# Branch projections, output projection and down product in rounds of four jobs, with pieces that roll through SBUF

## The chip, the cores and the metric

One core of a Trainium2 chip runs the whole kernel in one launch. The metric is the device time of that launch in microseconds. Five engines work side by side, each through its own queue in order: TensorE (PE in the profile, its weight loads PEld), VectorE (DVE), ScalarE (ACT), GpSimd (POOL) and SyncE (SP), which here issues the DMAs. SBUF is the memory on the chip, PSUM the eight banks that TensorE writes to, HBM the memory outside.

## The reference

One decoder layer on x, 1024 tokens by 1024 channels, float32:

```python
h = rmsnorm(x, norm_mix[l])
proj = h @ w_in
...
ys = jnp.stack([y_gla, y_mlstm, y_fox], axis=2)
branch = jnp.einsum('btnw,nwd->btnd', ys, w_branch)
g = jax.nn.sigmoid(gates.reshape(bsz, seq, N_BRANCH, D_MODEL) + b_gate)
merged = jnp.sum(branch * g, axis=2)
return merged @ w_out
...
h = rmsnorm(x, norm_ffn[l])
u = causal_dwconv(h @ w_up, conv_w, conv_b)
a, g = jnp.split(u, 2, axis=-1)
return (jax.nn.silu(g) * a) @ w_down
```

Both halves are added to x, and a last rmsnorm follows. Three token mixers (gated linear attention, mLSTM, forgetting attention) make the three ys from proj. The FFN's inner width is 2816, 22 blocks of 128.

## The kernel before

A large matrix product is a GEMM in jobs. A job takes 256 output channels: a two by two block product done with seven products instead of eight (Strassen in Winograd's form), numbered 1 to 7. Its stationary sides are a11, a12, a22 and four sums of blocks of the weights; its moving sides, the pieces, are two by two blocks of the activations and four differences of them. Every float32 operand is split into a high part (a cast on ScalarE) and a low part (a subtraction on VectorE, L151), and a product is three matmuls per 128 rows of depth: high by high, low by high, high by low. With four such depths a product has 12 matmuls of 128x512 and a job 84. `prep` (L1120) makes a product's weight sum on GpSimd (L1127) and splits it; it runs AHEAD = 2 products before `compute` (L1146), which does the matmuls (L143) and hands the PSUM bank to the job's `post` or `acc`. `products` (L51) sets the order: the seven products of a job, with products 3 and 4 of the job before between them.

From the start to some 1380 us run 48 input jobs and the mixers. Then come three branch GEMMs of four jobs (`merge_job` L1063: gate times branch output, summed over the branches into the tiles mg), the output projection (`out_half` L1261: plain, 768 matmuls of 256 columns, with the merged tiles split by `merged_split` L1082 as stationary), 22 up jobs, and the down product in three chunks of the inner width (6, 8 and 8 blocks) of four jobs each, added in SBUF into the rows acc (L1334).

The pieces of a branch or down GEMM are made by `combos` (L1022), a generator of seven steps. Each step loads blocks (tiles yb, T), takes differences (L1038, L1043, L1051, L1059; on VectorE, for the first chunk of down on GpSimd) and splits them into the slots b0 to b27. Step i hangs on the end of the i-th product of the last job of the GEMM before (`hook` L1362), so all seven fall into one job's time. A slot is written again once the last job has read the piece in it.

The norm at the start scales rows and turns them in one go: matmuls of x by a diagonal matrix dg (L226, `turn4` L229). The FFN norm turns rows that are already scaled (L1289, L147).

Each engine works through its queue in order, SP with its DMAs too, in an order fixed at build time; an instruction that waits holds up all behind it. A pool that is opened after another was closed takes its space: a first write to it waits until the last reader of the old tile is done.

Of the kernel before, what the change touches and what calls it, by code (L numbers as in the profile page):

```python
# [14 lines left out]
P = 128  # L15
T = 1024
# [19 lines left out]
MAP_IN = {1: 0, 5: 4, 6: 8, 2: 12, 7: 16, 3: 20, 4: 24}  # L36
MAP_FF = {1: 16, 2: 20, 5: 24, 6: 0, 7: 4, 3: 8, 4: 12}
# [3 lines left out]
class Job:  # L41
# [3 lines left out]
    def __init__(self, src1, src2, xc, post, name, nk=4, done=None, wide=False, acc=None):  # L45
        self.src, self.xc, self.post, self.name, self.nk = (src1, src2), xc, post, name, nk
        self.done, self.wide, self.acc = done, wide, acc
        self.raw, self.w, self.after = None, {}, {}

# [35 lines left out]

class Kern:
    def __init__(self, ctx, tc, a):
# [7 lines left out]
        self.swp = ctx.enter_context(tc.tile_pool(name="swp", bufs=1, reuse_waits="tile"))  # L95

# [39 lines left out]
    def slot(self, i, shape, dt, name):  # L136
        return self.big.tile(shape, dt, tag=f"b{i}", name=name)
# [14 lines left out]

    def unit(self, src, name="w"):
        raw = self.swp.tile([P, T], F32, tag="raw", name=f"{name}_raw", bufs=4)
        self.nc.sync.dma_start(out=raw, in_=src)
        out = []
        for i in range(2):
            hi = self.swp.tile([P, 512], F32R, tag="sh", name=f"{name}h", bufs=4)
            lo = self.swp.tile([P, 512], F32R, tag="sl", name=f"{name}l", bufs=4)
            self.split(raw[:, 512 * i:512 * i + 512], hi, lo)  # L160
            out.append((hi, lo))
        return out
# [52 lines left out]
    def norm(self, x, pool, vec):  # L215
# [9 lines left out]
        dg = pool.tile([P, P], F32, tag="dg", name="dg", bufs=4)  # L225
        nc.vector.tensor_scalar(dg, self.ident, sm[:, 2:3], None, op0=ALU.mult)  # L226
        return x, dg

    def turn4(self, xs, k):  # L229
        ps = self.pa()  # L230
        for i, x in enumerate(xs):
            o = ps[:, i * P:(i + 1) * P]
            if isinstance(x, tuple):
                self.mm(o, x[0][:, k * P:(k + 1) * P], x[1], True, True)
            else:
                self.tr(o, x[:, k * P:(k + 1) * P])
        return ps
# [14 lines left out]
    def put(self, xc, n, i, src, base, eng=None):  # L252
        t = self.slot(base[n] + i, [P, 2, 512], F32R, f"x{n}_{i}")
        self.split(src, t[:, 0, :], t[:, 1, :], eng)
        xc.setdefault(n, {})[i] = (t[:, 0, :], t[:, 1, :])

    def blocks1(self, xs, b, pool, gain, xc, base, qpool, qtag):
# [1416 lines left out]
```

## Time and profile before

| | |
|---|---|
| median of 3 runs | 2469.17 us (2462.83 to 2472.13) |
| profiled execution | 2460.64 us, span 2458.5 us |
| granted TensorE clock, mean | 0.983 |
| TensorE busy | 2333.9 us, 95% |
| VectorE busy | 1856.2 us, 75% |
| ScalarE busy | 1246.0 us, 51% |
| GpSimd busy | 903.8 us, 37% |
| DMA | 334.53 MB, 136 GB/s on the mean |

A busy share near 100% says that an engine always had something in hand, not that each instruction was as short as it can be; matmuls overlap, so their own durations sum to more than the time they take. What counts is the distance from one start to the next.

### The profile page before, as it was taken

How to read it: one execution, taken by the hardware profiler on the slowest of the kernel's cores; microseconds unless marked ns; L12 is line 12 of the kernel's file. 1: busy time of each engine (PE TensorE's matmuls, PEld its weight loads, DVE VectorE, ACT ScalarE, POOL GpSimd, SP SyncE). 2: the span in 40 equal slices, each digit the busy share in tenths (PEclk: the TensorE clock that was granted, in tenths of full speed). 3: DMA queues.
4: the chain of work that ended last, by engine and by line, in shares of the span. 5: the costliest groups of instructions: out<-in, count | busy, mean ns of one | idle time of the engine just before them, and what ended most of it. 6: DMA issues, size and time to landing. Idle time of an engine off the chain costs nothing. (4 is left out here: it accounts for less than half of the span.)

```text
span 2458.5 us, 34199 instructions
## 1 busy us (share of the span) xinstructions
PE 2333.9 (95%) x11531; PEld 1933.2 (79%) x11531; DVE 1856.2 (75%) x3180; ACT 1246.0 (51%) x2477; POOL 903.8 (37%) x892
## 2 busy tenths in 40 slices
PE   7999999989999999999999999899989999988898
PEld 6877778878888887888888777679878888876776
DVE  7687556767677775666778788864699998999885
ACT  5345455555566654555555643434455455553342
POOL 5322244444354452222222234551254433443322
PEclk9999999999999999999999999899989999999999
DMA  3355444554434444333443655434332222235442
GB/s 127 114 173 173 137 138 148 173 163 164 156 134 143 140 142 143 123 131 120 136 130 109 210 180 177 163 116 164 124 112 85 79 77 95 78 113 190 142 133 86
DMA packets 185743, 334.53 MB, mean 136 GB/s; under 512 B 17320, under 2 KB 79304, under 8 KB 185056
## 3 DMA queue, kind: packets, MB, share of 16 engines
q1 hardware_dynamic: 185568, 332.35, 40.9%
q8 instruction: 91, 1.49, 0.3%
q14 instruction: 84, 0.69, 0.1%
HBM read 236.70 MB, written 95.58 MB: 135 GB/s over the span
## 5 line engine op out<-in xcount | busy, mean ns | idle before, releaser
L143 PE MATMUL pg<-x,w6h 128*128 128x512 f32 x744 | 239.0, 400 | 12.7 <-DVE x L151 11.1
L143 PE MATMUL pg<-x,w7h 128*128 128x512 f32 x744 | 235.4, 397 | 2.6 <-ACT u L1155 2.5
L143 PE MATMUL pg<-x,w1h 128*128 128x512 f32 x744 | 236.0, 397 | 0.1
L143 PE MATMUL pg<-x,w4h 128*128 128x512 f32 x744 | 231.9, 392 | 3.1 <-DVE mt L1074 2.2
L143 PEld LDWEIGHTS pg<-x,w6h 128*128 128x128 f32 x744 | 140.4, 192 | 46.6 <-DVE x L151 15.3
L1127 POOL TENSOR_TENSOR sum<-up_raw 128x512 f32<-128x512 f32 x44 | 87.4, 1986 | 242.6 <-DMA up_raw<-in_w_up 201.0
L143 PE MATMUL pg<-x,w1l 128*128 128x512 f32 x372 | 148.7, 400 | 17.5 <-DVE w1l L151 17.5
L143 PEld LDWEIGHTS pg<-x,w7h 128*128 128x128 f32 x744 | 138.8, 191 | 33.1 <-ACT u L1155 4.6
L143 PEld LDWEIGHTS pg<-x,w4h 128*128 128x128 f32 x744 | 137.8, 188 | 33.1 <-issue 3.3
L143 PEld LDWEIGHTS pg<-x,w1h 128*128 128x128 f32 x744 | 140.0, 191 | 28.8 <-DVE x L151 0.5
L143 PE MATMUL pg<-x,w7l 128*128 128x512 f32 x372 | 147.2, 396 | 3.8 <-DVE w7l L151 3.8
L143 PE MATMUL pg<-x,w6l 128*128 128x512 f32 x372 | 147.1, 395 | 0.0
L143 PE MATMUL pg<-x,w4l 128*128 128x512 f32 x372 | 145.2, 390 | 1.0 <-DVE w4l L151 1.0
L1303 DVE SCALAR_TENSOR_TENSOR c<-u,cols,c 128x1022 f32<-128x1022 f32 x84 | 129.6, 1543 | 12.3 <-ACT c L1299 12.3
L150 ACT CAST w5h<-sum 128x512 fp32r<-128x512 f32 (+1 forms) x94 | 57.8, 615 | 131.0 <-PE pg L143 85.9
L143 PE MATMUL pg<-x,w5h 128*128 128x512 f32 x384 | 123.5, 401 | 0.4 <-DVE st L1234 0.3
L143 PE MATMUL pg<-x,w2h 128*128 128x512 f32 x384 | 121.6, 398 | 0.4 <-DVE st L1234 0.4
L143 PE MATMUL pg<-x,w3h 128*128 128x512 f32 x384 | 121.3, 395 | 0.0
L151 DVE TENSOR_TENSOR w5l<-sum,w5h 128x512 fp32r<-128x512 f32 (+1 forms) x94 | 87.9, 935 | 41.7 <-ACT w5h L150 35.4
L143 PE MATMUL pa<-x,w5h 128*128 128x512 f32 x360 | 114.4, 399 | 1.8 <-ACT w5h L150 0.9
L143 PE MATMUL pa<-x,w2h 128*128 128x512 f32 x360 | 111.2, 390 | 2.9 <-ACT w2h L150 2.9
L143 PE MATMUL pa<-x,w3h 128*128 128x512 f32 x360 | 113.7, 398 | 0.0
(481 smaller groups left out, 6881.3 us busy)
## 6 DMA issues: line engine op xcount, KB each, us to landing
up_raw<-in_w_up SPq DMA_DIRECT2D x44, 512.0 KB, 3.6
yb<-y_d SPq DMA_DIRECT2D x72, 256.0 KB, 3.5
yb<-in_w_dn SPq DMA_DIRECT2D x66, 256.0 KB, 3.2
gate_raw<-in_w_in SPq DMA_DIRECT2D x24, 512.0 KB, 3.6
g_d<-st SPq DMA_DIRECT2D x48, 256.0 KB, 2.2
br_raw<-in_w_br SPq DMA_DIRECT2D x24, 512.0 KB, 4.5
gth<-g_d SPq DMA_DIRECT2D x48, 256.0 KB, 2.6
f_d<-c SPq DMA_DIRECT2D x22, 512.0 KB, 2.9
```

The source lines that it names most:

```text
L143: self.nc.tensor.matmul(out, lhsT=lhsT, rhs=rhs, start=start, stop=stop, skip_group_check=skip)
L150: self.nc.scalar.copy(out=hi, in_=src)
L151: (eng or self.nc.vector).tensor_tensor(out=lo, in0=src, in1=hi.bitcast(F32), op=ALU.subtract)
L1127: self.nc.gpsimd.tensor_tensor(out=t, in0=a, in1=b, op=op)
L1303: nc.vector.scalar_tensor_tensor(out=c[:, s:], in0=u[:, :T - s], scalar=self.col("fw", 44 * tap + m), in1=c[:, s:], op0=ALU.mult, op1=ALU.add)
```

## The change

- The start norm scales x in place (rows in turns on VectorE and ScalarE) and turns it by PE transposes; the diagonal goes.
- Pieces live in seven groups of four tiles (g0 to g6). Branch GEMMs take five groups in rotation, the down chunks seven.
- Branch GEMMs, the output projection and the first two down chunks run in rounds: one product for all four jobs, then the next, in the order 1, 2, 5, 6, 3, 7, 4. Their weights lie in SBUF at once (pools `swp` and `wide`), their sums are made in place. The third chunk keeps the old order.
- A piece step hangs on the end of a round, about four rounds ahead of its use in the branches. For the branches after the first, differences 5 and 6 are on VectorE, 7 and 4 on GpSimd; for the first branch, the output projection and down all are on GpSimd.
- The output projection has four jobs of seven products, 336 matmuls of 512 columns; merged tiles are the stationary side, blocks of w_out the pieces, and x rows take the sum. `merged_split` and `out_half` go; `row_norm` does the norm of whole rows.
- The eight acc tiles are all in one pool that opens at the end of the FFN; the first adds wait for their loads.

```diff
+ORDER = (1, 5, 6, 2, 7, 3, 4)
+ROUND = (1, 2, 5, 6, 3, 7, 4)
+ROLL_BR = (0, 1, 2, 3, 4)
+ROLL_DN = (3, 0, 1, 4, 2, 5, 6)
...
+def rounds(jobs, ps=ROUND):
+
+    for p in ps:
+        for j in jobs:
+            yield j, p
...
+    def group(self, g, dt, name):
+
+        return self.big.tile([P, 4, 2, 512] if dt is F32R else [P, 4, T], dt, tag=f"g{g}", name=name)
...
-        dg = pool.tile([P, P], F32, tag="dg", name="dg", bufs=4)
-        nc.vector.tensor_scalar(dg, self.ident, sm[:, 2:3], None, op0=ALU.mult)
-        return x, dg
+        if vec:
+            nc.scalar.activation(x, x, AF.Copy, scale=sm[:, 2:3])
+        else:
+            nc.vector.tensor_scalar(x, x, sm[:, 2:3], None, op0=ALU.mult)
+        return x
     def turn4(self, xs, k):
         ps = self.pa()
         for i, x in enumerate(xs):
-            o = ps[:, i * P:(i + 1) * P]
-            if isinstance(x, tuple):
-                self.mm(o, x[0][:, k * P:(k + 1) * P], x[1], True, True)
-            else:
-                self.tr(o, x[:, k * P:(k + 1) * P])
+            self.tr(ps[:, i * P:(i + 1) * P], x[:, k * P:(k + 1) * P])
...
+    def combos(self, n, block, xc, base, order, ytile, ttile, engs):
+
...
+        for p in order:
+            for i in range(n):
+                if p == 1:
+                    src = load(0, i, 0)
+                elif p == 2:
+                    src = load(1, i, 0)
+                elif p == 3:
+                    src = load(1, i, 1)
+                elif p == 5:
+                    b = load(0, i, 0)
+                    src = ts[i] = ttile(i)
+                    nc.sync.dma_start(out=src, in_=block(0, i, 1))
+                    engs[p].tensor_tensor(out=src, in0=src, in1=b, op=ALU.subtract)
+                elif p == 6:
+                    b = load(1, i, 1)
+                    src = ts[i]
+                    engs[p].tensor_tensor(out=src, in0=b, in1=src, op=ALU.subtract)
+                elif p == 7:
+                    src = load(0, i, 0)
+                    engs[p].tensor_tensor(out=src, in0=ts[i], in1=src, op=ALU.subtract)
+                else:
+                    src = load(1, i, 0)
+                    engs[p].tensor_tensor(out=src, in0=src, in1=ts[i], op=ALU.subtract)
+                self.put(xc, p, i, src, base)
...
+    def out_job(self, env, p, xc, rows, done):
+
         nc = self.nc
+
+        def load(job):
+            mg = env["mg"]
+            for i in range(2):
+                rows[2 * p + i] = r = self.raw_tile(job, "x2")
+                nc.sync.dma_start(out=r, in_=self.a["x"][(2 * p + i) * P:(2 * p + i + 1) * P, :])
+            return [mg[kh][:, :, (2 * p + i) * P:(2 * p + i + 1) * P] for i in range(2) for kh in range(2)]
+
+        def acc(m, hf, b):
+            o = rows[2 * p + m][:, 512 * hf:512 * hf + 512]
+            nc.vector.scalar_tensor_tensor(out=o, in0=b, scalar=0.5, in1=o, op0=ALU.mult, op1=ALU.add)
+        return Job(None, None, xc, None, "wo", wide=True, acc=acc, load=load, done=lambda: done(p))
 
...
-            elif p == 7:
-                acc(1, 1, job.z)
+            elif p == 5 or p == 7:
                 acc(1, 1, b)
             elif p == 4:
...
+    def row_norm(self, pool, x, tt):
+        nc = self.nc
+        sm = pool.tile([P, 3], F32, tag="sm", name="sm", bufs=4)
+        junk = pool.tile([P, D], BF16, tag="junk", name="junk", bufs=1)
+        nc.sync.dma_start(out=self.x2_d[tt], in_=x)
+        nc.scalar.activation(junk, x, AF.Square, accum_out=sm[:, 0:1])
+        self.rsqrt(sm[:, 2:3], sm[:, 0:1], 1.0 / D, sm[:, 1:2], 1)
+        nc.vector.tensor_scalar(x, x, sm[:, 2:3], None, op0=ALU.mult)
...
+    def down_job(self, p, k0, nk, acc, wait, xc):
         nc = self.nc
 
         def add(m, hf, b):
-            o = acc[2 * p + m][:, 512 * hf:512 * hf + 512]
-            nc.vector.tensor_tensor(out=o, in0=o, in1=b, op=ALU.add)
+            def run():
+                o = acc[2 * p + m][:, 512 * hf:512 * hf + 512]
+                nc.vector.tensor_tensor(out=o, in0=o, in1=b, op=ALU.add)
+            if acc:
+                run()
+            else:
+                assert b is not None and hf == 0 and m == 0
...
+                jobs = wide([k.merge_job(env, n, b, p, x) for p in range(4)])
+                gemm.append((jobs, list(rounds(jobs)), x, branch_blocks(b),
+                             {5: V if n else G, 6: V if n else G, 7: G, 4: G}))
+            x = {}
+            jobs = wide([k.out_job(env, p, x, rows, ready.append) for p in range(4)])
+            seq = [(jobs[i], p) for h in ((0, 1), (2, 3)) for p in (1, 2) for i in h]
+            seq += list(rounds(jobs, (5, 6)))
+            seq += list(rounds(jobs[0:2], (3, 7, 4))) + list(rounds(jobs[2:4], (3, 7, 4)))
+            gemm.append((jobs, seq, x, out_blocks, {5: G, 6: G, 7: G, 4: G}))
+            steps, ends = [], []
+            m = 0
+            for jobs, seq, x, blocks, engs in gemm:
+                base = {}
+                for p in ROUND:
+                    base[p] = ROLL_BR[m % 5]
+                    m += 1
+                gen = k.combos(4, blocks, x, base, ROUND, ytile, ttile, engs)
+                steps += [gen] * 7
+                for p in ROUND:
+                    ends.append([q for q in seq if q[1] == p][-1])
+            for i, gen in enumerate(steps):
+                job, p = (ins[-1], ORDER[i]) if i < 5 else ends[i - 5]
+                after(job, p, lambda gen=gen: next(gen))
+            yield from products(ins, LEADS)
+            yield None, 0
+            for jobs, seq, x, blocks, engs in gemm:
+                for j in jobs:
+                    j.held = env["wide"]
+                yield from seq
...
+                last = c == len(chunks) - 1
+                x = {}
+                ds = [k.down_job(p, k0, nk, acc, wait, x) for p in range(4)]
+                ps = ORDER if last else ROUND
+                base = {p: ROLL_DN[i] for i, p in enumerate(ps)}
+                gen = k.combos(nk // 2, dn_blocks(c), x, base, ps,
+                               lambda: k.swp.tile([P, 512], F32, tag="ws", name="yb", bufs=3),
+                               lambda i: k.swp.tile([P, 512], F32, tag="sc", name="T", bufs=4),
+                               {5: G, 6: G, 7: G, 4: G})
+                steps += [gen] * 7
+                if last:
+                    for p, j in enumerate(ds):
+                        j.second = p % 2 == 1
+                        j.done = lambda p=p: dn["done"].extend((2 * p, 2 * p + 1))
+                    seqs.append((ds, products(ds)))
+                else:
+                    wide(ds)
+                    seqs.append((ds, rounds(ds)))
+                    ends += [(ds[-1], p) for p in ROUND]
+            for gen, (job, p) in zip(steps, ends):
...
             nfin = ep.tile([P, D], F32, name="nfin")
-            for i in range(2, 8):
+            for i in range(8):
                 acc.append(ep.tile([P, D], F32, name=f"acc{i}"))
-                k.nc.sync.dma_start(out=acc[i], in_=k.x2_d[i])
-            k.nc.sync.dma_start(out=nfin, in_=a["norm_final"].partition_broadcast(P))
-            dn["done"] = []
+                nc.sync.dma_start(out=acc[i], in_=k.x2_d[i])
+            for f in wait:
+                f()
```

VectorE in the middle of the branches, first before, in the last job of the first branch: x7 and the like are pieces, w3l and the like low parts of weights, mt and mg belong to the merge.

```order
L1051 TENSOR_TENSOR yb_16238<-T_16061,yb_16238 128x512
L1077 SCALAR_TENSOR_TENSOR mg7_15647<-gth_16233,mt_16235 128x512
L1051 TENSOR_TENSOR yb_16244<-T_16067,yb_16244 128x512
L151 TENSOR_TENSOR x7_0_16241<-yb_16238,x7_0_16241 128x512
L1051 TENSOR_TENSOR yb_16250<-T_16073,yb_16250 128x512
L151 TENSOR_TENSOR x7_1_16247<-yb_16244,x7_1_16247 128x512
L1051 TENSOR_TENSOR yb_16256<-T_16079,yb_16256 128x512
L151 TENSOR_TENSOR x7_2_16253<-yb_16250,x7_2_16253 128x512
L151 TENSOR_TENSOR w3l_16265<-sum4_16262,w3h_16264 128x512
L151 TENSOR_TENSOR x7_3_16259<-yb_16256,x7_3_16259 128x512
L151 TENSOR_TENSOR w6l_16286<-sum2_16283,w6h_16285 128x512
L151 TENSOR_TENSOR w4l_16305<-br_raw_15952,w4h_16304 128x512
```

Now, in the round of product 3 of the second branch:

```order
L1076 TENSOR_TENSOR mt_16671<-u2_16576,pa_16466 128x512
L166 TENSOR_TENSOR w7l_16700<-sum1_16389,w7h_16699 128x512
L1079 SCALAR_TENSOR_TENSOR gth_16669<-gth_16669,mt_16671 128x512
L1076 TENSOR_TENSOR mt_16694<-u2_16595,pa_16487 128x512
L166 TENSOR_TENSOR w7l_16723<-sum1_16414,w7h_16722 128x512
L1079 SCALAR_TENSOR_TENSOR gth_16692<-gth_16692,mt_16694 128x512
L1051 TENSOR_TENSOR T_16746<-T_16746,yb_16744 128x512
L1051 TENSOR_TENSOR T_16754<-T_16754,yb_16752 128x512
L1076 TENSOR_TENSOR mt_16717<-u2_16614,pa_16507 128x512
L1051 TENSOR_TENSOR T_16761<-T_16761,yb_16759 128x512
L1079 SCALAR_TENSOR_TENSOR gth_16715<-gth_16715,mt_16717 128x512
L1051 TENSOR_TENSOR T_16768<-T_16768,yb_16766 128x512
```

Before, four differences, their four splits and a single job's weights stand in one product after another; now the merge of four jobs, four weights and four differences of a single piece group share a round.

SP at the start of the down product, before (acc0 and acc1 stand 90 rows earlier):

```order
L1314 DMA f_d_115<-c_22428 128x1024
L1027 DMA yb_22951<-in_w_dn 128x512
L1314 DMA f_d_115<-c_22633 128x1024
L1115 DMA dn_raw_22781<-f_d_115 128x6x128
L1535 DMA acc2_22689<-x2_d_114 128x1024
L1535 DMA acc3_22691<-x2_d_114 128x1024
L1535 DMA acc4_22693<-x2_d_114 128x1024
L1535 DMA acc5_22695<-x2_d_114 128x1024
L1535 DMA acc6_22697<-x2_d_114 128x1024
L1535 DMA acc7_22699<-x2_d_114 128x1024
```

and now:

```order
L1310 DMA f_d_115<-c_22000 128x1024
L1036 DMA yb_22109<-in_w_dn 128x512
L1036 DMA yb_22114<-in_w_dn 128x512
L1036 DMA yb_22118<-in_w_dn 128x512
L1601 DMA acc0_22060<-x2_d_114 128x1024
L1601 DMA acc1_22062<-x2_d_114 128x1024
L1601 DMA acc2_22064<-x2_d_114 128x1024
L1601 DMA acc3_22066<-x2_d_114 128x1024
L1601 DMA acc4_22068<-x2_d_114 128x1024
```

The loads of acc stood behind the last f_d store for six rows; now for all eight, and three piece loads stand between.

VectorE around the first add into acc, now (the last f, L1309 on tile c, stands five rows ahead of the first row; x4 and x1 are pieces of the first and second chunk):

```order
L166 TENSOR_TENSOR x4_21986<-yb_21989,x4_21986 128x512
L166 TENSOR_TENSOR x4_21986<-yb_21994,x4_21986 128x512
L166 TENSOR_TENSOR w5l_22159<-sum1_22156,w5h_22158 128x384
L166 TENSOR_TENSOR x1_22111<-yb_22109,x1_22111 128x512
L166 TENSOR_TENSOR w5l_22176<-sum1_22173,w5h_22175 128x384
L166 TENSOR_TENSOR x1_22111<-yb_22114,x1_22111 128x512
L166 TENSOR_TENSOR w5l_22210<-sum1_22207,w5h_22209 128x384
L166 TENSOR_TENSOR x1_22111<-yb_22118,x1_22111 128x512
L1331 TENSOR_TENSOR acc0_22060<-acc0_22060,pg_22018 128x512
L166 TENSOR_TENSOR w5l_22227<-sum1_22224,w5h_22226 128x384
L1331 TENSOR_TENSOR acc0_22060<-acc0_22060,pa_22130 128x512
L1331 TENSOR_TENSOR acc2_22064<-acc2_22064,pg_22043 128x512
```

Before, five adds into acc0 and acc1 stood ahead of the last f; now the first add stands 13 rows behind it, and the adds of four jobs follow together.

## Rows read from the trace of the kernel before

**Rows 1.** The page: busy us of each engine, share of the span, instructions

```profile
PE 2333.9 (95%) x11531; PEld 1933.2 (79%) x11531; DVE 1856.2 (75%) x3180; ACT 1246.0 (51%) x2477; POOL 903.8 (37%) x892
```

**Rows 2.** Stages: us, TensorE busy (instructions), granted clock, DMA share, GB/s

```profile
1380.00:1659.00 279.00, 253.73 (x1068) 0.97 0.52 170
1659.00:1760.00 101.00, 97.29 (x799) 1.00 0.47 163
1760.00:1803.00 43.00, 33.56 (x140) 0.84 0.09 32
1803.00:2165.00 362.00, 362.00 (x1599) 1.00 0.28 93
2165.00:2440.00 275.00, 249.00 (x1032) 0.96 0.43 137
```

**Rows 3.** TensorE in time, output projection: start us, us, operation

```profile
1744.78 0.28 PE L143 MATMUL pg<-woh,mh 128*128 128x256 f32 x1
1744.90 0.28 PE L143 MATMUL pg<-wol,mh 128*128 128x256 f32 x1
```

**Rows 4.** TensorE in time, entry of the FFN; last, a stage

```profile
1771.17 4.23 PE L147 MATMUL pa<-cst,x 128*128 128x128 f32 x32
...
1785.18 0.63 PE L143 MATMUL pg<-x,w6l 128*128 128x512 f32 x1
1785.61 0.63 PE L143 MATMUL pg<-x,w6h 128*128 128x512 f32 x1
...
1784.00:1798.00 14.00, 8.20 (x17) 0.52 0.00 0
```

**Rows 5.** Waits of TensorE, branches: us in total, times, longest us

```profile
PE pa L143 <- DVE w5l L151: 4.6, 1, 4.6
```

**Rows 6.** Waits of TensorE, down product

```profile
PE pg L143 <- DVE w1l L151: 11.3, 5, 3.9
```

**Rows 7.** Stages: VectorE busy us (instructions); last, GpSimd

```profile
1380.00:1659.00 279.00, 230.19 (x312) 0.97 0.52 170
1820.00:2160.00 340.00, 309.88 (x288) 1.00 0.27 92
2165.00:2440.00 275.00, 237.70 (x316) 0.96 0.43 137
...
1380.00:1659.00 279.00, 128.88 (x79) 0.97 0.52 170
```

**Rows 8.** VectorE in time; GpSimd in time beside it; VectorE later without it

```profile
1781.10 1.76 DVE L273 TENSOR_TENSOR t<-b,t 128x512 f32<-128x512 f32 x1
1782.78 1.75 DVE L151 TENSOR_TENSOR x<-t,x 128x512 fp32r<-128x512 f32 x1
...
1782.28 1.71 POOL L284 TENSOR_TENSOR b<-b,t 128x512 f32<-128x512 f32 x1
...
1797.78 0.68 DVE L151 TENSOR_TENSOR w5l<-sum,w5h 128x512 fp32r<-128x512 f32 x1
1798.38 0.68 DVE L151 TENSOR_TENSOR w3l<-sum,w3h 128x512 fp32r<-128x512 f32 x1
```

**Rows 9.** SP in time, loads of acc; last, their landing

```profile
2233.92 0.33 SPq L1314 DMA_DIRECT2D f_d<-c  x1
...
2234.90 3.32 SPq L1535 DMA_DIRECT2D acc<-x_d  x6
...
DMA to landing us min/median/max: 2.6/2.7/9.6
```

**Rows 10.** VectorE in time, convolution at the end of the FFN

```profile
2226.33 1.27 DVE L1303 SCALAR_TENSOR_TENSOR c<-u,cols,c 128x1022 f32<-128x1022 f32 x1
```

**Rows 11.** TensorE in time, start; last, a later VectorE group

```profile
10.28 10.52 PE L143 MATMUL pa<-dg,x 128*128 128x128 f32 x64 [10.28 <-DVE dg L226]
...
35.73 4.80 PE L143 MATMUL pa<-dg,x 128*128 128x128 f32 x26 [2.94 <-DVE dg L226]
...
L1289 DVE TENSOR_SCALAR x<-x,sm 128x1024 f32<-128x1024 f32 x6 | 4.5, 752 | 7.9 <-DMA x_d<-x 7.6 <-POOL sm L167 0.3
```

More of the change, by code (lines that the diff above doesn't have):

```diff
@@ L1194, in compute, with gemms @@
             f()
-    def gemms(self, jobs, lead=0):
-        seq = products(jobs, lead)
+    def gemms(self, seq):
         due = []
@@ L1394, in body, with ytile @@
[L1394 to L1405 removed]
+        env = {}
+        rows = {}
+        V, G = nc.vector, nc.gpsimd
+        def ytile():
+            return env["cmb"].tile([P, 512], F32, tag="yb", name="yb", bufs=4)
@@ L1443, in body @@
                 pass
-        with pool("mrg") as gp:
-            mrg["pool"] = gp
-            while ("g", 23) not in k.written:
-                next(stream)
-            stage.close()
-            gr = right.enter_context(pool("mg", side="right"))
-            mrg["mg"] = mg = [gr.tile([P, T], F32, name=f"mg{j}") for j in range(8)]
-            for _ in stream:
-                pass
-            k.merged_split(mg, (6, 7), mh, ml)
-        right.close()
+        env["wide"] = k.raw2 = left.enter_context(pool("wide"))
+        env["cmb"] = cmb.enter_context(pool("cmb"))
+        while ("g", 23) not in k.written:
+            next(stream)
+        stage.close()
+        late = ctx.enter_context(ExitStack())
+        env["late"] = late.enter_context(pool("late", side="right"))
+        env["mg"] = [k.group(g, F32, f"mg{g}") for g in (5, 6)]
+        for _ in range(3 * 28):
+            next(stream)
+        late.close()
+        lp = right.enter_context(pool("lead", side="right"))
         xc = {}
-        lp = right.enter_context(pool("lead", side="right"))
         bg = []
@@ L1483, in ffn @@
         def ffn():
             jobs = list(k.ffn_jobs(xc, tiles, bg))
-            last = jobs[-1]
+            seqs, steps, ends = [], [], [(jobs[-1], p) for p in ORDER]
             for c, (k0, nk) in enumerate(chunks):
-                hook(last, Lazy(lambda c=c: down_combos(c, xcs[c])))
-                for p in range(4):
-                    jobs.append(k.down_job(p, k0, nk, acc, xcs[c]))
-                    if c == len(chunks) - 1:
-                        jobs[-1].done = lambda p=p: dn["done"].extend((2 * p, 2 * p + 1))
-                last = jobs[-1]
@@ new lines, in ffn @@
+            yield from products(jobs, LEADS)
+            for ds, seq in seqs:
+                for job, p in seq:
+                    if p not in (1, 2):
+                        job.held = dn["pool"]
+                    yield job, p
+        ff = k.gemms(ffn())
+        for _ in range(12):
+            next(stream)
+        cmb.close()
+        with pool("oh", side="right") as hp:
+            while len(ready) < 2:
+                next(stream)
+            for tt in range(4):
+                k.row_norm(hp, rows[tt], tt)
+            next(stream)
+            b = k.blocks0([rows[tt] for tt in range(4)], hp, "nf")
+            next(stream)
+            for p in (1, 2):
+                for i in range(4):
+                    k.put(xc, p, i, b[i + 4 * (p - 1)], MAP_FF)
+            for _ in stream:
+                pass
+            for tt in range(4, 8):
+                k.row_norm(hp, rows[tt], tt)
+            for _ in range(2 * LEADS):
+                next(ff)
+            for _ in k.blocks1([rows[tt] for tt in range(4, 8)], b, hp, "nf", xc, MAP_FF,
+                               lambda i: k.swp.tile([P, 512], F32, tag="sc", name="b22", bufs=4),
+                               lambda i: env["wide"].tile([P, 512], F32, tag="S", name="t1", bufs=4)):
+                pass
```

295 lines of the change are left out of this document (104 added, 191 removed).

## Prediction, written before the result was known

> **What bounds the kernel now.** I read the busy shares first, then a table of stages, then TensorE's waits in the stages that the change touches, and last single rows for prices. TensorE is busy 95% of a span of 2458.5 us, VectorE 75% [rows 1]. That is an average over stages. In the table of stages [rows 2] the up projection of the FFN, 1803 to 2165 us, is filled: 1599 matmuls in 362.0 us, never idle, so one 512-column matmul costs 362.0/1599 = 0.2264 us. With that price the other stages show what they lose:
> - branches, 1380 to 1659 us: 279.0 - 1068 x 0.2264 = 37.2 us;
> - down product, 2165 to 2440: 275.0 - 1032 x 0.2264 = 41.4 us;
> - output projection, 1659 to 1760: its 256-column matmuls follow each other every 0.12 us [rows 3], so 768 x 0.12 = 92.2 us, and 32 transposes at 4.23/32 = 0.13 us [rows 4] make 4.2; 101.0 - 96.4 = 4.6 us lost;
> - entry of the FFN, 1760 to 1803: 43.0 - 108 x 0.2264 - 4.2 = 14.3 us.
> In branches and down product TensorE waits for VectorE's low halves of weights (w5l, w1l) [rows 5, 6], and VectorE is busy 230.2 of 279 and 237.7 of 275 us [rows 7]. The piece steps all hang on the last job of the GEMM before, so VectorE's work comes in heaps while its average fits.
>
> **The change part by part.**
> Branches. TensorE's work stays (12 jobs x 84 matmuls; a branch is 336 x 0.2264 = 76.1 us). On VectorE a branch now has 28 subtractions for pieces, 28 for weights, 28 in the merges, and 8 piece differences in the first two branches: 92, 92, 84. GpSimd has 24, 40 and 48 operations (16 weight sums, 8 or 16 piece differences, 16 merge adds from the second branch on). Back to back a VectorE operation comes every 0.60 us [rows 8]. What one GpSimd operation adds to VectorE I take from the stage itself: 312 operations x 0.60 = 187.2 of the 230.2 us busy, so 43.0/79 = 0.54 us each [rows 7]. That gives 55.2 + 13.0 = 68.2, 55.2 + 21.6 = 76.8 and 50.4 + 25.9 = 76.3 us against 76.1: 0.9 us over. Rounds are uneven (the one of p3 and the one of p7 carry 16 to 24 VectorE operations in 12 x 4 x 0.2264 = 10.9 us), but pieces run four rounds ahead and weights three products, so I book 3 us a branch, 9. At each of the two boundaries between branches 4 MB of weights come within about two rounds (21.7 us), beside pieces and gates of some 5 MB; DMA moved 170 GB/s at a share of 0.52 [rows 2], so 327 GB/s when full, and 9 MB take 27.5 us; most has a round to spare, and I book 3 us each, 6. Lost 16 instead of 37.2: **gain 21**. Ends: 6 lost (gain 31) if the lead hides the unevenness; at the dearest row for GpSimd beside VectorE [rows 8], where one operation of each takes 1.68 us together (1782.78 - 1781.10), the price is 1.68 - 0.60 = 1.08 us, VectorE needs 81.1, 98.4 and 102.2, that is 53.4 over TensorE, 68 lost (gain -31). I take 0.54, since it is the mean of these very operations.
>
> Output projection. 336 matmuls x 0.2264 = 76.1 us for 92.2: 16.1 less. The moving pieces are made during the last branch (counted above), the split of the merged tiles (16 operations on VectorE) goes, and its stationary is cast like any weight. Without the merged split the start has no chain of its own; I book 3 us lost for 4.6. **Gain 17.7**; ends 12 (a chain through the last merge, as long as the longest wait of rows 5, twice) and 20.
>
> Entry of the FFN. The norm now is one Square of 1024 and one scaling of 1024 per row instead of four pieces, and blocks1 stays: 32 transposes, then a chain of VectorE and GpSimd in turns at half TensorE clock (0.52) [rows 4]. I see no operation leave this chain, so 14.3 stay; ends 10 and 20. **Gain 0**.
>
> Down product. Its piece differences go to GpSimd: of 316 VectorE operations 32 leave, 284 x 0.60 = 170.4; GpSimd has 48 sums and 44 differences, x 0.54 = 49.7; 220 us against 1032 x 0.2264 = 233.6, so on average VectorE is no bound (at 1.08 it would be 269.8, 36 over). What stays is the start. All eight acc tiles now share a pool that opens when the FFN's is released, so no add can run before the last f is stored. In the order on SP the loads stand behind that store and three loads of pieces, where before acc0 and acc1 had been there long. Before: store issued 2233.92, acc loads from 2234.90, 3.32 us to issue six, landing after 2.6 to 9.6 us [rows 9]. Rounds p1 and p2 fill all eight PSUM banks in 2 x 36 x 0.2264 = 16.3 us, and p5 needs one that an add frees. From the first w1l of the down product to the last f VectorE has 23 operations, 6 of them products of the convolution at 1.27 us [rows 10], the rest at 0.60, and 12 more stand between the last f and the first add: 6 x 1.27 + 29 x 0.60 = 25.0 us, 8.7 late. The loads would be there by then: 17.8 to the last f, 1.0 to the first load, 1.4 for three other loads ahead of it, 2.7 to land, 22.9. With four such adds in a row, landings up to the worst and matmuls at half clock after the idle I book 18 for the start and 4 for the other rounds, 22 instead of 41.4: **gain 19**. Ends: 10 lost (gain 31), 54 lost at price 1.08 (gain -13).
>
> Start. 64 products by the diagonal take two records each, the first 64 records 10.52 us [rows 11]; 64 transposes are one record each at 0.13 us. After the first four tiles the last 26 records (4.80 us) halve: 2.4. Against that a scaling of 1024 columns, 0.75 us on VectorE [rows 11], stands where a diagonal of 128 was scaled: 0.5 to 0.8 late by estimate. **Gain 2**; ends -3 (products after the transposes at half clock: 0.43 us spacing as at 1785.18 to 1785.61 in rows 4) and 5.
>
> Sum: 21 + 17.7 + 0 + 19 + 2 = 59.7, about 60 us. The profiled execution took 2460.64 us (span 2458.5): 2400.6. It lies 8.5 us under the median 2469.17, so I predict **2409** on the median's scale.
>
> **A rule that speaks against it.** The rows at 1781 to 1788 us show VectorE at 1.75 us beside GpSimd at 1.71, one started as the other nears its end, while alone VectorE takes 0.68 [rows 8]. The Trainium skill, page "SBUF — State Buffer", section "Who interferes with whom", says why: the two share a port as an exclusive lock, and a VectorE operation with two SBUF inputs stands still for a whole GpSimd operation. By this rule nearly every subtraction here would pay, and moving differences to GpSimd would cost as much as it saves: the sum would be that of the slower rival below. The trace agrees in those rows, while the mean of the branches, 0.54 us, is half of that, and with it the sum is the 60 us above.
>
> **Rivals.**
> Partly locked: the moved differences read and write SBUF at both operands, next to more subtractions in the same rounds, and the price becomes 0.75 us. Between 0.54 and 1.08 the sum falls from 60 to 21 - 52, 17.7, 0, 19 - 32, 2, that is -24: 84 us over 0.54, so 0.75 costs 33. Gain 27, 2442. For it: rows 8; against it: rows 7.
> Slower: the same mechanism at its full price. VectorE becomes the bound of branches two and three (98.4 and 102.2 us against 76.1) and of the down product (269.8 against 233.6); time 2460.6 + 24 = 2485, on the median's scale 2493. It decides from a price of 0.54 + 0.54 x 60/84 = 0.93 us on. For it: rows 8. Against it: in the filled FFN stage GpSimd's weight sums ran beside a VectorE busy 309.9 of 340 us, and TensorE lost nothing [rows 2, 7].
> All stalls go: the lead of whole rounds hides unevenness and loads, branches lose 6, down product 10. Gain 82, 2387. For it: the filled stage, with VectorE at 91% (309.9/340) [rows 2, 7]. Against it: the acc loads behind the last f, which nothing shortens.
> Late acc: each bank waits until 9.6 us after the eighth load, and half clock follows; 10 to 15 us of the gain go: 2419 to 2424, inside the likeliest case's range.
>
> **How the numbers follow.** Likeliest case 0.60, its own range 2393 to 2428 (the two large terms each off by a third, and the late acc). All stalls gone 0.14. Partly locked 0.15. Slower 0.06. No measurable change, where losses meet somewhere between, 0.05. About 0.5%, 12 us, is what a measurement of this kernel can tell from no change; the partly locked case lies mostly beyond it (0.13 of 0.15). Faster 0.60 + 0.14 + 0.13 = 0.87; same 0.07; slower 0.06. The range reaches from the case without stalls, 2383, to the partly locked one at a price of 0.80, 2452.
>
> **What would show it.** Branch GEMMs of 76 to 82 us each, matmuls 0.2264 apart, TensorE's waits on w1l and w5l under 5 us together; VectorE's extra per GpSimd operation near 0.54. The output projection as 336 matmuls of 512 columns in 76 to 80 us. In the down product one wait of 5 to 15 us before the first p5 matmul, released by an acc add, and little after it. It is wrong if the branch rounds of p3 and p7 last over 13 us each, if waits on pieces (x) come up in place of weights, or if the first add comes over 20 us after the last f.

## The result and the profile after

The changed kernel is slower: 2486.46 us (median of 5 runs, 2485.20 to 2493.76) against 2466.69 (5 runs), ratio 1.0085 with a 95% interval of 1.0064 to 1.0106. The prediction was 2409, range 2383 to 2452, with 0.06 on slower. It was wrong in sign. Medians are of fast runs: one of five runs of the kernel dnv below, 2610 us at a granted clock of 0.839, was slow and is left out.

The page gives the busy time of each engine, its share of the span and its instructions; beside [rows 1] the span is 29.6 us longer (2488.1), TensorE is busy 9 us less, VectorE 56 us and GpSimd 150 us more.

```profile
PE 2324.9 (93%) x11035; PEld 1903.4 (77%) x11035; DVE 1911.8 (77%) x3108; ACT 1245.8 (50%) x2441; POOL 1053.5 (42%) x988
```

The stages of the changed kernel, cut where TensorE is at the same matmul as in [rows 2] (us, TensorE busy and instructions, granted clock, DMA share, GB/s):

```profile
1375.00:1674.00 299.00, 261.20 (x1068) 0.93 0.59 197
1674.00:1760.00 86.00, 80.42 (x358) 0.98 0.26 92
1760.00:1808.00 48.00, 37.90 (x153) 0.82 0.13 44
1808.00:2170.00 362.00, 362.00 (x1599) 1.00 0.27 88
2170.00:2470.00 300.00, 250.02 (x1029) 0.92 0.43 140
```

Priced like the kernel before: the branches have the same 1068 matmuls in 299.0 us, so 299.0 - 241.8 = 57.2 are lost where 37.2 were; the down product loses 300.0 - 1029 x 0.2264 = 67.0 where 41.4 were. Output projection and entry of the FFN together take 134 us where 144 were taken, the up projection 362.0 as before, and the start gives 5 (the first weights of the last input job are cast at 1349.4 us, before at 1354.4; the twelve kernels with the changed start spread from 1347.1 to 1354.0, so the 5 is rough). The sum, +20.0 + 25.6 - 10 - 5 = 30.6, is the span's difference within 1 us.

TensorE's waits in the branches, beside [rows 5] (total, times, longest, us):

```profile
PE pg L158 <- DVE w6l L166: 9.7, 2, 5.0
PE pg L158 <- DVE w7l L166: 7.0, 2, 4.1
PE pg L158 <- ACT w1h L165: 5.5, 2, 4.3
PE pg L158 <- DVE mt L1076: 5.1, 1, 5.1
```

It still waits for low parts of weights, but now for those of the rounds of p6 and p7. These two rounds of the second branch (48 matmuls, 10.9 us when filled):

```profile
1520.10:1538.20 18.10, 13.39 (x49) 0.81 0.49 156
1549.10:1566.70 17.60, 13.50 (x49) 0.81 0.54 175
```

A round loses more than its wait: behind 4.7 us without work in the p6 round the matmuls start 0.43 us apart, the half clock, before they are back at 0.23. The waits in the down product, beside [rows 6]:

```profile
PE pg L158 <- ACT w7h L165: 12.1, 1, 12.1
PE pg L158 <- DVE acc L1331: 9.6, 2, 7.4
PE pa L158 <- DVE acc L1331: 9.3, 1, 9.3
```

Three are new: one of 12.1 us inside the last up job, and the adds into acc. VectorE and then GpSimd in both stages, beside [rows 7] (busy us, instructions):

```profile
1375.00:1674.00 299.00, 257.32 (x282) 0.93 0.59 197
2170.00:2470.00 300.00, 240.97 (x285) 0.92 0.43 140
...
1375.00:1674.00 299.00, 187.26 (x118) 0.93 0.59 197
2170.00:2470.00 300.00, 148.03 (x102) 0.92 0.43 140
```

VectorE is busy 257.3 of 299 us: on average there is room. By the prediction's division a GpSimd operation now costs it (257.3 - 282 x 0.60)/118 = 0.75 us, not 0.54.

VectorE in time, and at the end GpSimd beside it, around the p6 round of the second branch (start, us, operation, in brackets the idle time before it):

```profile
1519.86 1.47 DVE L1079 SCALAR_TENSOR_TENSOR gth<-gth,mt 128x512 f32<-128x512 f32 x1 [3.97 <-DMA gth<-g_d]
...
1524.72 4.66 DVE L166 TENSOR_TENSOR w6l<-sum,w6h 128x512 fp32r<-128x512 f32 x4
1529.30 4.68 DVE L166 TENSOR_TENSOR x<-yb,x 128x512 fp32r<-128x512 f32 x4
...
1517.00 1.28 POOL L1154 TENSOR_TENSOR sum<-sum,br_raw 128x512 f32<-128x512 f32 x1
...
1525.54 6.68 POOL L1154 TENSOR_TENSOR sum<-br_raw,sum 128x512 f32<-128x512 f32 x4 [2.50 <-DVE w6l L166]
```

VectorE first stands idle for a gate, then does four weights and four pieces in 9.3 us. The rows are means: beside a GpSimd sum one of them took 1.76 to 1.78 us, without one 0.68. TensorE waits 4.7 us for w6l here. Two readings fit: the gate's load is late and all behind it too, or both engines are full and stand in each other's way.

TensorE at the start, beside [rows 11]: 

```profile
9.49 1.30 PE L162 MATMUL pa<-cst,x 128*128 128x128 f32 x5 [9.49 <-DMA cst<-in_consts]
...
13.32 4.08 PE L162 MATMUL pa<-cst,x 128*128 128x128 f32 x17 [0.56 <-ACT x L230]
...
17.05 0.78 PE L158 MATMUL pg<-x,w1h 128*128 128x512 f32 x1
```

The first product begins at 17.05 us, between the transposes, where 64 records of diagonal products kept TensorE until 20.80.

### The profile page after: what moved, and what is told of

Same layout as the page of the kernel before. It is cut to its first block, busy times and chain, and to the rows that moved or that the text cites. A ratio compares the mean times of both kernels' runs of the same rounds, so it can differ in the third digit from the quotient of the medians.

```text
span 2488.1 us, 33203 instructions
## 1 busy us (share of the span) xinstructions
PE 2324.9 (93%) x11035; PEld 1903.4 (77%) x11035; DVE 1911.8 (77%) x3108; ACT 1245.8 (50%) x2441; POOL 1053.5 (42%) x988
## 5 line engine op out<-in xcount | busy, mean ns | idle before, releaser
L158 PE MATMUL pg<-x,w6h 128*128 128x512 f32 x776 | 251.7, 403 | 20.0 <-DVE x L166 12.5
L158 PE MATMUL pg<-x,w7h 128*128 128x512 f32 x776 | 250.1, 404 | 14.6 <-ACT w7h L165 12.1
L158 PE MATMUL pg<-x,w1h 128*128 128x512 f32 x776 | 248.2, 400 | 9.8 <-ACT w1h L165 5.5
L158 PE MATMUL pg<-x,w4h 128*128 128x512 f32 x776 | 244.6, 396 | 12.3 <-DVE mt L1076 5.1
L1154 POOL TENSOR_TENSOR sum<-up_raw 128x512 f32<-128x512 f32 x44 | 90.7, 2062 | 228.8 <-DMA up_raw<-in_w_up 194.7
L158 PEld LDWEIGHTS pg<-x,w7h 128*128 128x128 f32 x776 | 148.7, 195 | 47.0 <-ACT w7h L165 12.8
L158 PE MATMUL pg<-x,w7l 128*128 128x512 f32 x388 | 156.9, 404 | 10.9 <-DVE w7l L166 10.9
L166 DVE TENSOR_TENSOR x<-yb,x 128x512 fp32r<-128x512 f32 x135 | 136.3, 1044 | 23.8 <-ACT x L165 22.3
L165 ACT CAST x<-yb 128x512 fp32r<-128x512 f32 x135 | 79.6, 619 | 97.7 <-POOL yb L1061 35.6
L158 PE MATMUL pa<-x,w2h 128*128 128x512 f32 x392 | 122.0, 392 | 4.8 <-ACT w2h L165 4.8
L166 DVE TENSOR_TENSOR w5l<-sum,w5h 128x512 fp32r<-128x512 f32 (+1 forms) x98 | 97.9, 999 | 35.6 <-ACT w5h L165 31.9
```

The lines of the kernel that those rows point to most:

```text
L158: self.nc.tensor.matmul(out, lhsT=lhsT, rhs=rhs, start=start, stop=stop, skip_group_check=skip)
L165: self.nc.scalar.copy(out=hi, in_=src)
L166: (eng or self.nc.vector).tensor_tensor(out=lo, in0=src, in1=hi.bitcast(F32), op=ALU.subtract)
L1154: self.nc.gpsimd.tensor_tensor(out=t, in0=a, in1=b, op=op)
```

## The experiments

Each kernel was timed in three rounds beside the kernel before. The table has its median, its ratio to that kernel with the 95% interval, and two lengths that hold all that the change touches: **middle**, from the first weight cast of the last input job to that of the third up job (branches, output projection, entry), and **down**, from the first weight cast of the last up job to the end.

| kernel | us | ratio (95%) | middle | down |
|---|---|---|---|---|
| before | 2465 to 2470 | 1 | 449.5 | 292.8 |
| changed | 2486.5 | 1.0085 (1.0064 to 1.0106) | 458.4 | 318.5 |
| gth4 | 2485.7 | 1.0071 (1.0046 to 1.0095) | 455.5 | 316.4 |
| olddn | 2475.4 | 1.0030 (1.0018 to 1.0042) | 456.2 | 304.1 |
| accearly | 2480.6 | 1.0057 (1.0038 to 1.0076) | 454.7 | 310.9 |
| dn0ring | 2489.4 | 1.0092 (1.0075 to 1.0109) | 454.7 | 314.2 |
| brv | 2474.7 | 1.0029 (1.0017 to 1.0042) | 440.3 | 317.4 |
| dnv | 2477.8 | 1.0035 (1.0014 to 1.0055) | 457.0 | 305.3 |
| allv | 2453.7 | 0.9943 (0.9925 to 0.9961) | 438.7 | 300.9 |
| nopool | 2429.7 | 0.9849 (0.9816 to 0.9882) | 419.2 | 292.1 |
| beforev | 2438.2 | 0.9871 (0.9849 to 0.9893) | 433.2 | 285.3 |
| rings | 2434.2 | 0.9854 (0.9837 to 0.9871) | 422.5 | 294.6 |
| entryv | 2424.7 | 0.9815 (0.9798 to 0.9832) | 415.9 | 292.6 |
| best | 2427.5 | 0.9821 (0.9798 to 0.9843) | 415.0 | 299.0 |

Five kernels with the changed middle lie between 454.7 and 458.4, three with the changed down product between 316.4 and 318.5; differences of under 4 us in one profile tell nothing. The intervals of the ratios reach 3 to 8 us to each side.

**gth4: more gate buffers.**

```diff
-            th = pool.tile([P, 512], F32, tag="gth", name="gth", bufs=2)
+            th = pool.tile([P, 512], F32, tag="gth", name="gth", bufs=4)
```

> The changed kernel with four buffers for the gate tile gth instead of two; nothing else. Theory A (queues and rings: in the rounds of p6 and p7 of the second and third branch VectorE stands idle in front of the merge until its gate is loaded, 6.2 and 9.8 us, the weights' low parts queue behind it, and the gate's load waits on SP for a buffer, 33.7 and 30.5 us): the p6 rounds lose under 2 us each instead of 7, p7 some less, 10 to 20 us faster than the changed kernel, about 2466 to 2476 us. Theory B (VectorE beside GpSimd is the bound, the price of a GpSimd operation rose): the operations are the same, so the time stays within 4 us of 2486.

No gain. The gate's wait on VectorE is gone, and the time is not. VectorE in that kernel, then GpSimd, in the same place:

```profile
1505.78 0.67 DVE L1076 TENSOR_TENSOR mt<-s,pa 128x512 f32<-128x512 f32 x1
1506.38 1.18 DVE L166 TENSOR_TENSOR w5l<-sum,w5h 128x512 fp32r<-128x512 f32 x1
1507.48 1.78 DVE L1079 SCALAR_TENSOR_TENSOR gth<-gth,mt 128x512 f32<-128x512 f32 x1
...
1512.58 6.87 DVE L166 TENSOR_TENSOR x<-yb,x 128x512 fp32r<-128x512 f32 x4
1519.37 6.82 DVE L166 TENSOR_TENSOR w6l<-sum,w6h 128x512 fp32r<-128x512 f32 x4
...
1505.27 1.74 POOL L1061 TENSOR_TENSOR yb<-yb,T 128x512 f32<-128x512 f32 x1
...
1522.21 6.87 POOL L1154 TENSOR_TENSOR sum<-br_raw,sum 128x512 f32<-128x512 f32 x4
```

Now VectorE never idles there, and eight subtractions take 13.6 us, 1.70 each, beside GpSimd operations of 1.7: one of each per 1.70 us, the pair of [rows 8]. The gate was late because GpSimd's merge adds, which free its buffer, were late: in the changed kernel the loads of gates stand 64.2 us on SP behind them. Only mt escapes: 0.67 us at 1505.78 though GpSimd runs; its second operand comes from PSUM. Theory A falls for the branches.

**olddn: the down product as before.** The down chunks run in the order of `products` again, with the steps on one job, differences on VectorE from the second chunk on, and acc0 and acc1 early:

```diff
-                    seqs.append((ds, rounds(ds)))
+                feed(last, gen)
...
+            yield from products(jobs, LEADS)
```

> The changed kernel with the down product as before: jobs one after another, all seven piece steps on the last job of the GEMM before, differences on VectorE from the second chunk on, acc0 and acc1 loaded early, own tiles for blocks and differences. Start, branches and output projection stay changed. If the loss of the down product (67 us without work on TensorE from 2170 us on, against 41 before) is its own: 24 to 28 us faster than the changed kernel, about 2460 us, a little under before. If it comes from what is ahead of it (the end of the FFN shifted against the pieces), under 10 us.

The median is 11 us lower and down falls by 14.4, not by 24 to 28; down still takes 11 us more than the same order in the kernel before. Here pieces live in whole groups of four, which are free only once all four are read, and the FFN ends differently; which of them holds the 11 us was not tried.

**accearly: three acc tiles early.**

```diff
+                    for i in (0, 2, 4):
+                        acc[i] = k.raw2.tile([P, D], F32, name=f"acc{i}")
+                        nc.sync.dma_start(out=acc[i], in_=k.x2_d[i])
```

> The changed kernel with acc0, acc2 and acc4 loaded during the up jobs, so that the first adds of three of the four jobs need not wait for the end of the FFN. Theory A1 (the first add behind the last f and the loads is the price of rounds at the down product's start): the wait of 9.3 us on the first adds goes to under 2 us, 8 to 12 us faster with the half clock behind it, about 2475 us. Theory A2 (the pieces of the first chunk are late by themselves, since blocks and differences share rings of three and four tiles with the up jobs): TensorE then waits for pieces or weights at the same place, under 4 us faster.

Down falls by 7.6 and the median by 5.9, less than the 8 to 12 that A1 said and more than A2 allowed. TensorE's waits in its down product:

```profile
PE pg L158 <- ACT w7h L165: 13.4, 2, 11.8
PE pg L158 <- DVE acc L1331: 8.7, 2, 7.1
PE pa L158 <- DVE w2l L166: 4.7, 1, 4.7
```

The wait of 9.3 us on pa is gone, with 4.7 for a weight in its place; the one of the last up job stays.

**dn0ring: own tiles for the first down chunk.**

```diff
-                               lambda: k.swp.tile([P, 512], F32, tag="ws", name="yb", bufs=3),
+                               lambda c=c: (k.swp.tile([P, 512], F32, tag="ws", name="yb", bufs=3) if c else
+                                            dn["first"].tile([P, 512], F32, tag="yb", name="yb", bufs=3)),
```

(and the same for T)

> The changed kernel with tiles of their own for the first down chunk: three for blocks (yb) and three for differences (T), instead of the rings that the last up jobs use for weight sums and kept banks. Theory A2 (shared rings): the wait of 12.1 us in the last up job for w7h goes, 12 to 18 us faster, 2468 to 2474 us. Theory B (VectorE and GpSimd are saturated there): within 4 us of 2486. Theory A1 alone (acc): the last up job is whole but the wait on acc grows by as much, under 4 us faster.

No gain. The wait for w7h went, and came back a little later:

```profile
PE pa L158 <- DVE w2l L166: 10.5, 3, 6.5
PE pg L158 <- ACT x L165: 7.8, 1, 7.8
PE pa L158 <- DVE acc L1331: 7.5, 1, 7.5
```

In this kernel shared rings are where the wait shows, not what the time hangs on. A2 falls.

**brv and dnv: the differences back on VectorE.**

```diff
-                             {5: V if n else G, 6: V if n else G, 7: G, 4: G}))
+                             {5: V, 6: V, 7: V, 4: V}))
...
-            gemm.append((jobs, seq, x, out_blocks, {5: G, 6: G, 7: G, 4: G}))
+            gemm.append((jobs, seq, x, out_blocks, {5: V, 6: V, 7: V, 4: V}))
```

> The changed kernel with the piece differences of the branches and of the output projection on VectorE, 48 operations moved from GpSimd. Theory L (where both engines have work, one operation of each takes 1.70 us together, since each stands still for the other, so a GpSimd operation costs VectorE 1.08 us and an operation moved saves 1.08 - 0.60 = 0.48): up to 23 us, of which the stalls of the rounds p6, p7 and p4 give back 10 to 23: 2463 to 2476 us. Theory M (the mean price of 0.54 us holds): VectorE gets 48 x 0.06 = 3 us more work, time within 4 us of 2486. Theory A (loads and rings): within 4 us of 2486 too.

```diff
-                               {5: G, 6: G, 7: G, 4: G})
+                               {5: V, 6: V, 7: V, 4: V})
```

> The changed kernel with the piece differences of the down product on VectorE, 44 operations moved from GpSimd. Theory L: up to 21 us; 10 to 21 us faster, 2465 to 2476 us. Theory M: within 4 us of 2486. Theory A (rings of three blocks, which free a block only after the difference, cast and subtraction): 3 to 8 us faster, because a difference takes 0.6 us instead of 1.7 in that chain.

Each shortens its own stage and leaves the other: middle falls by 18.1 (440.3), down by 13.2 (305.3). By these lengths both lie where L put them, though the busier engine got more work. The medians, 2474.7 and 2477.8, agree for brv and lie two above the range for dnv. M is out, and A for the branches. For the down product A (3 to 8 us) is out by the 13.2 us of the stage alone; the median's 8.7 us lies at its edge. The branches of brv, TensorE and GpSimd, over the same matmuls as the changed kernel's:

```profile
1378.00:1667.00 289.00, 257.59 (x1067) 0.95 0.63 203
...
1378.00:1667.00 289.00, 129.75 (x80) 0.95 0.63 203
```

They lose 289.0 - 1067 x 0.2264 = 47.4 us where 57.2 were lost. The other 8 us of the middle are behind them: the 7.2 us that the output projection lost at its first weights are gone.

**allv and nopool: the other GpSimd operations too.** allv is both, with accearly and

```diff
-                nc.gpsimd.tensor_tensor(out=o, in0=o, in1=th, op=ALU.add)
+                nc.vector.tensor_tensor(out=o, in0=o, in1=th, op=ALU.add)
```

nopool adds

```diff
-            self.nc.gpsimd.tensor_tensor(out=t, in0=a, in1=b, op=op)
+            (self.nc.vector if job.inplace else self.nc.gpsimd).tensor_tensor(out=t, in0=a, in1=b, op=op)
```

> The changed kernel with the piece differences of branches, output projection and down product and the merge's adds on VectorE, and with acc0, acc2 and acc4 loaded during the up jobs. GpSimd keeps the weight sums. Theory L: 23 + 21 + 32 x 0.48 = 15 us, and 6 for the acc tiles, up to 65 us; 45 to 60 us faster than the changed kernel, 2426 to 2441 us. Theory M: 124 operations x 0.06 us more work on VectorE, no gain but that of the acc tiles, about 2480 to 2490 us.

> As the kernel with all differences and merge adds on VectorE, and the weight sums of the jobs in rounds on VectorE too (48 in the branches, 16 in the output projection, 32 in the down product): no GpSimd operation stands beside VectorE in a round. VectorE has 132 operations x 0.60 = 79.2 us in a branch against 76.1 on TensorE. Theory L: again 96 x 0.48 = 46 us less on VectorE, so 10 to 20 us faster than with the sums on GpSimd, 2410 to 2428 us. Theory M: 3 to 6 us of VectorE more than TensorE in each branch, 5 to 15 us slower than with the sums on GpSimd.

allv misses: 2453.7, 13 us above its range; for the merge adds the middle shows 1.6 of the 15 us (438.7 after 440.3), less than profiles differ. Moving the last ones, the sums, brought 24, above L's 10 to 20, 19.5 of it in the middle; the time, 2429.7, is still 2 above L's range. L's 0.48 us an operation does not hold step by step. My reading is that as long as a weight sum stands in a round on GpSimd, the weight behind it waits a pair's time: TensorE waits 10.5 us for w7l in the branches of allv, and in nopool that wait is not among its rows. The branches of nopool over the same matmuls as the changed kernel's: TensorE, VectorE, GpSimd.

```profile
1373.00:1642.50 269.50, 251.50 (x1067) 0.97 0.67 221
...
1373.00:1642.50 269.50, 246.16 (x404) 0.97 0.67 221
...
1373.00:1642.50 269.50, 0.00 (x0) 0.97 0.67 221
```

404 operations in 246.2 us, 0.61 each: with no GpSimd beside it VectorE is back at the price of [rows 8], and with 122 operations more than the changed kernel (404 for 282) it is busy 11 us less (246.2 for 257.3). TensorE loses 269.5 - 1067 x 0.2264 = 27.9 us. The rounds of p6, p7 and p4 of the second branch:

```profile
1506.70:1517.60 10.90, 10.90 (x50) 1.00 0.43 130
1528.40:1539.70 11.30, 11.29 (x50) 1.00 0.51 154
1539.70:1557.40 17.70, 13.64 (x49) 0.81 0.82 261
```

p6 and p7 are whole now; p4 still loses 6.9 us, here and in the third branch, with a wait for w4l. Sums (L1154) and subtractions in a row, around the p6 round:

```profile
1505.22 1.94 DVE L166 TENSOR_TENSOR w6l<-sum,w6h 128x512 fp32r<-128x512 f32 x3
...
1511.89 1.89 DVE L1154 TENSOR_TENSOR sum<-br_raw,sum 128x512 f32<-128x512 f32 x3
```

**beforev: the kernel before, without GpSimd in these stages.** Its order, slots and output projection stay; sums of branch and down jobs, merge adds and the first chunk's differences go to VectorE.

```diff
-            self.nc.gpsimd.tensor_tensor(out=t, in0=a, in1=b, op=op)
+            (self.nc.vector if job.name in ("br", "dn") else self.nc.gpsimd).tensor_tensor(out=t, in0=a, in1=b, op=op)
```

> The kernel before, with its order of jobs, its piece slots and its output projection, but with the weight sums of branch and down jobs, the merge's adds and the differences of the first down chunk on VectorE. Theory L1 (the pairing of GpSimd and VectorE costs the kernel before as well, and 37 + 41 us of its stalls hang on it): 79 + 67 GpSimd operations x 0.48 = 70 us less on VectorE in these stages, 15 to 30 us faster than before, 2435 to 2450 us. Theory L2 (there the heaps of piece steps on one job are the limit; GpSimd stood still when VectorE was busy): within 6 us of 2467.

L1: 2438.2, inside its range of 2435 to 2450. It lies 8.5 us above nopool, with intervals of the ratios that overlap. Branches and down product:

```profile
1380.00:1645.00 265.00, 250.12 (x1069) 0.98 0.58 184
2153.00:2420.00 267.00, 247.62 (x1030) 0.96 0.44 141
```

The branches lose 265.0 - 1069 x 0.2264 = 23.0 us where nopool's rounds lose 27.9; down takes 285.3 against 292.1. So of the stalls that the rounds were to remove, 37.2 and 41.4 us, a part hung on GpSimd: 14 us in the branches and 8 in the down product (267.0 - 1030 x 0.2264 = 33.8 are left). Without GpSimd the rounds gain nothing in either stage; they lose some 5 and 7 us more than the old order. What nopool is ahead, it owes to the output projection with the entry, 124 us for 142, and to the start.

**rings, entryv, best.** rings is nopool with dn0ring in place of the early acc tiles; entryv is nopool with the eight differences at the FFN's entry on VectorE:

```diff
-            nc.gpsimd.tensor_tensor(out=b[i], in0=t1[i], in1=b[i], op=ALU.subtract)
+            (nc.gpsimd if gain == "nm" else nc.vector).tensor_tensor(out=b[i], in0=t1[i], in1=b[i], op=ALU.subtract)
```

> The kernel without GpSimd operations in the rounds, but with tiles of its own for blocks and differences of the first down chunk (three and three) in place of the early acc tiles. Theory A2 (with VectorE free of pairs the last up job waits for a slot of the ring that weight sums and blocks share, 10.4 us, and the first w1l behind the pieces, 10.5 us): both waits shrink to under 4 us, the acc wait comes back with 5 to 9: 5 to 15 us faster than 2430. If the rings are no limit: 5 to 10 us slower, by the acc tiles.

> The kernel without GpSimd operations in the rounds, and with the eight GpSimd differences at the entry of the FFN on VectorE. Theory L: there eight pairs of 1.68 us follow each other; on VectorE they are 16 operations x 0.60 = 9.6 us for 13.4: 3 to 6 us faster (TensorE also runs at half clock behind them). Theory M: 8 x 0.06 us, no change.

> Both: tiles of its own for the first down chunk and the entry's differences on VectorE, no GpSimd operation in the rounds. Sum of the two single steps, 2410 to 2425 us.

rings has a median 4.5 us above nopool's, with intervals that overlap, so nothing is gained. The wait for w7h is gone, but the one for w1l stays (10.3 us) and the one on acc is back (7.0): rings alone are no limit, a second time. entryv's median is 5.0 us below nopool's, again with overlapping intervals; the middle bears it out, 415.9 and 415.0 with the entry on VectorE (entryv, best) against 419.2 and 422.5 without (nopool, rings). VectorE there, beside the 1.75 us of [rows 8]:

```profile
1749.00 0.69 DVE L278 TENSOR_TENSOR t<-b,t 128x512 f32<-128x512 f32 x1
1749.60 0.69 DVE L166 TENSOR_TENSOR x<-t,x 128x512 fp32r<-128x512 f32 x1
```

best, with rings in it, is no better than entryv. entryv, 2424.7 us, beats both kernels: 1.85% under the one before (1.68 to 2.02).

## Why the prediction was wrong

- **The step that failed** is the price: "What one GpSimd operation adds to VectorE I take from the stage itself ... 0.54 us each", and with it "on average VectorE is no bound". In the rounds GpSimd's work comes where VectorE's does: for p5 and p6 it has four piece differences, eight sums and four merge adds, 16 operations that at 1.70 us take 27 us in two rounds of 10.9 (in the second branch 28.0, from 1504.20 to 1532.23 us). Eleven of these 16 took 1.60 to 1.76 us, beside VectorE operations of up to 1.78; five took 1.28 to 1.36. The row with the true price of a pair, 1.68 us, stood in [rows 8] and was kept as the far end.
- It was not only the number. The stage's mean did rise, to 0.75 us in the branches, which is the price of the partly locked rival; its sum gives 2442, still 44 us short. A mean over the stage has long stretches in it with one engine alone, so it can't tell what a round costs where both are full.
- The branches were to lose 16 and lost 57.2. Over the same matmuls nopool loses 27.9, so 29 of the 41 us that were missing went with GpSimd's operations. No run separates the pairs from GpSimd's own slowness: at 1.28 us alone, the 16 operations would still fill 20.5 of the 21.8 us.
- Uneven rounds were booked at 3 us a branch, 9 in all. The rounds p5 to p4 lost 5.8, 16.8 and 17.3 us in the three branches, 39.9 in all, and 18.3 in nopool, so this term was half its size even without GpSimd. "Weights three products" ahead was no cover: the low parts stand in VectorE's queue behind the merge and the pieces of their round. Of the signs named ahead, the p7 rounds took 15.6 to 17.6 us, over the 13; the p3 rounds took 10.9, and it was p6 that took 18.1 and 17.6.
- The loads at the first boundary were mispriced on their own: 3 us were booked at each of the two later ones, which lost nothing in their p1 rounds, while the first branch's p1 round took 20.0 us for 38 matmuls, 11.4 too much, with seven weight loads issued only from 1392 to 1399 us, behind the pieces on SP. The 11.4 is in part spread: in four other kernels with the same branches (olddn, accearly, dn0ring, dnv) it is 4.6 to 7.1. In brv and nopool 3.3 and 3.2 stay; no run tells it apart further.
- The output projection gained 16.1 us of matmul time as forecast; with the entry the two gained 10, not 17.7, for stalls at its first weights (7.2 us, none in brv) and at the entry.
- The down product was to lose 22 and lost 67.0. Its wait on acc, 9.3 us for 8.7, agrees by luck. By the prediction the first add comes 25.0 us after the first w1l and the rounds p1 and p2 take 16.3; in the trace the add comes 40.1 us after it (2210.26 to 2250.34) and the rounds take 27.1. VectorE and TensorE were both late, by nearly the same time:

```profile
2210.26 0.55 DVE L166 TENSOR_TENSOR w1l<-dn_raw,w1h 128x384 fp32r<-128x384 f32 x1
...
2250.34 0.67 DVE L1331 TENSOR_TENSOR acc<-acc,pg 128x512 f32<-128x512 f32 x1
```

- Early acc tiles give back 7.6 us of the down product (accearly), the piece differences 13.2 (dnv). With the sums of the rounds off GpSimd too (26 operations are left on it), nopool still loses 273.0 - 1028 x 0.2264 = 40.3 there, and two waits near its start make half of it:

```profile
2129.00:2402.00 273.00, 244.17 (x1028) 0.94 0.47 149
...
PE pg L158 <- DVE w1l L166: 10.5, 1, 10.5
PE pg L158 <- ACT w7h L165: 10.4, 1, 10.4
```

So 18 us over the 22 booked come neither from acc nor from the operations moved; what holds them stays open. In rings, with own tiles, the wait for w7h goes and the other stays.
- The start gained some 5 where 2 were booked, within a spread as large.
- The slower rival had the mechanism, and its total (2493 for 2486) is right in part by luck: it had 68 lost in the branches for 57.2 and 54 in the down product for 67.0. It stood at 0.06 because the filled FFN stage was read as evidence against it; there four sums a job stand beside TensorE's 19 us, and, as I read it, a pair's price is hidden. Its words "VectorE becomes the bound" were not right: VectorE was idle over 40 of 299 us, and what the rows show to bind is the chain of pairs in single rounds, p6 and p7 above all. The range's ends don't follow from its own terms: the case without stalls is 2387 and a price of 0.80 gives 2449, for 2383 and 2452. The rows speak first: pairs of 1.70 us, and mt at 0.67. The Trainium skill, page "SBUF — State Buffer", section "Who interferes with whom", has the rule (a VectorE instruction with two SBUF inputs against a GpSimd one that reads SBUF, none with one such input); the rows agree with both halves of it.

## What to carry to other kernels

Price work on two engines that get in each other's way at the pair's time wherever both will have it in the same stretch, and draw that stretch, not the stage: a mean over a stage with idle time in it is a lower bound. An engine with a low busy share is not a free place to move work to; here 404 operations on VectorE and none on GpSimd cost TensorE 27.9 us over the same matmuls, 282 and 118 cost it 57.2. Before a reordering is credited with a stall, take away the suspected cost in the old order too: beforev, in the old order, had 1.3 of the 1.5% that nopool gained.

## What the runs showed of the hardware that was not expected

A GpSimd sum of 128x512 takes 1.28 us alone (1517.00 above) and 1.70 beside VectorE, so in a pair both lose: VectorE 1.1 us, GpSimd 0.4. The same sum on VectorE takes 0.6 (L1154 above: three in 1.89 us). Adds with one operand in PSUM (mt) kept 0.67 us beside GpSimd.
